# Sample queries and keys projected during the LRU out-projection, out-projection chunks in the order 2, 0, 1, and the first attention head's tiles loaded in the gate path

## Chip, core and metric

One NeuronCore of one Trainium2 chip. The metric is the device time of one execution in microseconds (us), lower is better; for a kernel on one core this is the span of its instructions and about 1.6 us around it.

## What is computed

One inference step of a decoder trunk of four layers, for a prompt of 1024 tokens and for 8 sample sequences of 4 new tokens each (32 rows), all in float32. Layer 0 and 3 are gated convolutions, layer 1 is an RG-LRU, layer 2 is differential attention with a paged cache of 2048 past tokens for each sample sequence. Cut to what matters here:

```python
for i in range(4):
    up = xp * (1 + scale_p) + shift_p        # prompt  (1, 1024, 1024)
    us = xs * (1 + scale_s) + shift_s        # sample  (8, 4, 1024)
    if i == 1:
        op, osm = rglru(up) @ r_w_out, rglru(us) @ r_w_out
    if i == 2:
        q, k, v, z = split(u @ d_w_in)       # 1024 columns each; q and k rotated
        o = softmax(q k_past.T, q k_new.T) @ v    # 8 heads, two score maps each
        o = subln(o) * silu(z) @ d_w_out
    xp = layer_norm(alpha * xp + gate_p * op)
    xs = layer_norm(alpha * xs + gate_s * osm)
```

The sample rows are attended against `cache_k` and `cache_v` (64 MB each is read), the prompt rows against themselves.

## The kernel before

Tokens are columns: 1024 prompt tokens and 32 sample tokens in three chunks of 384, 384 and 288 columns (`CH`); the sample tokens are the last 32 columns of chunk 2. Every large product is made of three float32r products (high x high, high x low, low x high), so a chunk of one output block is 24 matmuls (`gemm_chunk`, L127).

`boundary` closes a layer: `out_proj` multiplies chunk 0, 1, 2 by the eight column blocks of the output weights (eight gemms of 24 matmuls for each chunk), adds the residual that it reads back from DRAM (`xr`, L284), and yields the chunk; `norm` then transposes it, takes the statistics, and `modulate` transposes it back and writes the next layer's input `u` in two parts and, for layer 2, the sample columns once more into `self.us` (L260). The weights (`wo`) are loaded while the first chunk is computed. All weights pass through a ring of two raw buffers of 512 KB (`raw`, tag "raw"): a DMA fills one, ScalarE and VectorE split it into high and low part (L111, L112; L1003, L1004), and only then is the buffer free for the next DMA.

`attn_layer` follows. `qkv` makes six passes of 512 columns (q, q, k, k, v, v); each has eight prompt tiles of 128 tokens, 24 matmuls of 512 columns each (L1060), and loads the next pass's weights meanwhile. In the first pass, after tiles 1 to 4, it also fetches the weights of passes 0 to 3 a second time, raw (`wq_0s` to `wq_3s`, L992, 16 DMAs of 512 KB), multiplies the sample rows with them (`sample_half`, L1012, products in 32-column groups of the array, four instructions for each DMA), sums the four groups with a matmul by `sel` (`sample_rows`, L1036), rotates, and transposes into `qsb` and `ksb`. Beside `qkv`, a second generator `sample_keys` reads the pages of `cache_k` (POOL's queue, 256 DMAs of 256 KB), transposes them on VectorE (`kt`, L1444) and multiplies them with the sample queries (`sps`, L1388) in 16 bursts. `merge` interleaves the two by estimated costs. `zpath` makes the gate (`zz`, 24 chunks), still beside `sample_keys`. Then `heads` does the prompt attention, head by head: it loads keys and queries of a head twice into raw tiles (`tok`, L1150), values `V` (L1157), splits them on ScalarE and POOL (`ks`, `qhl`), and beside it `sample_values` reads `cache_v` (`vp`, 128 DMAs of 512 KB on SP's queue) and multiplies (`sacc`, L1492).

The order on each engine is not the program's. The tile framework takes the instructions with the program's order as priority and lets a simulated timeline choose the next ready one for each engine; it fixes the order before the run, and each engine and each DMA queue then runs it strictly in order. Buffers are handed out in program order within a ring. PSUM banks are handed out by `deal`: three banks P, one Q, three R, one U.

## Time and profile before

| | us |
|---|---|
| time, median of 3 runs | 2441.85 (2439.98 to 2446.5) |
| the profiled execution | 2443.42 |
| its span | 2441.8 |
| PE busy | 2297.3 (94%) |
| VectorE (DVE) busy | 1469.6 (60%) |
| ScalarE (ACT) busy | 910.1 (37%) |
| POOL busy | 341.7 (14%) |

The stretches of the span that this document is about: the LRU's out-projection from 817 to 920, `qkv` from 920 to 1382, `zpath` to 1510, `heads` from 1510 to about 1880, all in us from the span's start. A busy share is read together with the idle time and its releaser: an engine that is idle elsewhere costs nothing, and PE's own idle time does.

### The profile page before, as it was taken

What the parts mean: (1) busy time and instruction counts of PE and PEld (TensorE: products, weight loads), DVE (VectorE), ACT (ScalarE), POOL (GpSimd) and SP (SyncE); (2) the same over time, 40 slices, a digit from 0 to 9 for tenths busy, and PEclk for the clock granted to TensorE, in tenths of its full rate; (3) what the DMA queues carried; (4) which work ended last, traced back from release to release, by engine and by line L of the source; (5) the groups of instructions that cost most, each with busy time, mean ns of one, the idle gap of its engine ahead of it and who ended that gap; (6) DMA issues with size and microseconds to landing.
All of it is one profiled execution on the core that took longest, in us unless ns stands there. A gap on an engine that the chain in (4) does not pass through costs nothing.

```text
span 2441.8 us, 45387 instructions
## 1 busy us (share of the span) xinstructions
PE 2297.3 (94%) x17288; PEld 1952.8 (80%) x17288; DVE 1469.6 (60%) x3047; ACT 910.1 (37%) x1874; POOL 341.7 (14%) x541
## 2 busy tenths in 40 slices
PE   7999999999999998998989997889898999999997
PEld 4989999997888995466656786555566999999997
DVE  5866665467555555555654553676676477666655
ACT  4333333245555233111111111666665254333410
POOL 0200000001010001222223222333321000000000
PEclk9999999999999998999999998999999999999999
DMA  9243335334344425656768765999992321222442
GB/s 327 80 141 105 96 113 164 119 97 124 119 138 130 147 83 185 211 180 211 234 200 271 235 216 170 294 283 293 294 320 87 100 93 53 70 62 71 123 132 75
DMA packets 289392, 393.42 MB, mean 161 GB/s; under 512 B 18749, under 2 KB 197054, under 8 KB 289174
## 3 DMA queue, kind: packets, MB, share of 16 engines
q1 hardware_dynamic: 268694, 323.40, 43.3%
q0 software_dynamic: 20480, 67.13, 8.8%
q8 instruction: 136, 2.23, 0.4%
q14 instruction: 82, 0.67, 0.1%
HBM read 331.14 MB, written 59.31 MB: 160 GB/s over the span
## 4 chain that ended last, share of the span: by engine, by line
PE 67%; issue 13%; DMA 10%; POOLq 4%; DVE 2%; POOL 2%; ACT 1%; SPq 1%; DVEq 0%; ACTq 0%
PE op L127 15%; PE inX L605 12%; PE inZ L605 6%; DMA vp<-cache_v 4%; PE xb L127 4%; PE z L127 4%; PE in L127 3%; POOLq L1347 3%; PE inY L605 3%; PE ada L195 3%; DMA tok<-qd 2%; PE in L726 2%; PE in L641 2%; PE qk L1060 2%; PE zz L127 2%
## 5 line engine op out<-in xcount | busy, mean ns | idle before, releaser
L1060 PE MATMUL qk<-wq,ua 128*128 128x512 f32 x1152 | 289.6, 408 | 2.5 <-DVE wq L1004 2.5
L1060 PEld LDWEIGHTS qk<-wq,ua 128*128 128x128 f32 x1152 | 218.8, 193 | 72.1 <-issue 18.2
L1444 DVE STREAM_TRANSPOSE kt<-kp 128x512 f32<-128x512 f32 x256 | 171.3, 696 | 127.4 <-DMA kp<-cache_k 95.1
L1354 POOL DMA_DIRECT2D kp<-cache_k x256 | 140.4, 548 | 391.8 <-DVE kt L1444 262.5
L1177 PE MATMUL S<-ks,qhl 128*128 128x512 f32 (+2 forms) x384 | 109.9, 396 | 24.5 <-issue 12.3
L1229 ACT ACTIVATE P<-S,rr 128x512 f32<-128x512 f32 (+2 forms) x192 | 110.5, 581 | 49.7 <-DVE rr L1217 26.7
L287 DVE SCALAR_TENSOR_TENSOR r<-op,gate,xr 128x384 f32<-128x384 f32 (+1 forms) x96 | 54.3, 570 | 116.8 <-PE op L127 79.6
L1177 PEld LDWEIGHTS S<-ks,qhl 128*128 128x128 f32 x384 | 61.3, 198 | 60.1 <-ACT P L1229 24.6
L1492 PE MATMUL sacc<-vp,pv 128*16 128x256 f32 x1024 | 81.2, 395 | 24.1 <-DMA vp<-cache_v 23.8
L127 PEld LDWEIGHTS z<-ub,wrz 128*128 128x128 f32 x576 | 92.6, 188 | 11.7 <-issue 10.1
L127 PE MATMUL z<-ub,wrz 128*128 128x384 f32 (+1 forms) x576 | 98.2, 326 | 0.0
L1064 ACT ACTIVATE qkr<-qk 128x512 f32<-128x512 f32 x48 | 28.4, 594 | 186.1 <-PE qk L1060 146.9
L127 PEld LDWEIGHTS zz<-ua,wz 128*128 128x128 f32 x576 | 93.6, 190 | 3.6 <-issue 3.4
L127 PE MATMUL zz<-ua,wz 128*128 128x384 f32 (+1 forms) x576 | 96.1, 326 | 0.0
L1270 PEld LDWEIGHTS pv<-V,wt 128*128 128x128 f32 x576 | 75.8, 198 | 23.0 <-ACT wt L1262 11.6
L127 PEld LDWEIGHTS xb<-ub,wrx 128*128 128x128 f32 x504 | 80.9, 188 | 12.7 <-issue 9.2
L1388 PE MATMUL sps<-kt,qbd 32*32 32x512 f32 x2048 | 86.2, 625 | 4.1 <-DVE kt L1444 2.7
L1270 PE MATMUL pv<-V,wt 128*128 128x128 f32 x576 | 84.5, 289 | 4.3 <-ACT wt L1262 3.6
L324 POOL TENSOR_TENSOR rs<-mv,mhalf 128x1 f32<-128x1 f32 (+1 forms) x36 | 19.2, 540 | 494.5 <-DVE mv L322 489.0
L127 PE MATMUL xb<-ub,wrx 128*128 128x384 f32 (+1 forms) x504 | 87.8, 328 | 0.0
L195 PE MATMUL ada<-wada,ct 128*32 128x512 f32 x384 | 82.5, 616 | 4.3 <-DMA wada<-w_ada 3.1
L127 PE MATMUL op<-ub,ua 128*128 128x384 f32 (+1 forms) x504 | 85.5, 326 | 0.0
(488 smaller groups left out, 5176.0 us busy)
## 6 DMA issues: line engine op xcount, KB each, us to landing
kp<-cache_k POOLq DMA_DIRECT2D x256, 256.0 KB, 3.7
vp<-cache_v SPq DMA_DIRECT2D x128, 512.0 KB, 10.0
wada<-w_ada SPq DMA_DIRECT2D x96, 512.0 KB, 4.2
xa<-xat SPq DMA_DIRECT2D x64, 192.0 KB, 2.2
wra<-a_w_in SPq DMA_DIRECT2D x24, 512.0 KB, 4.1
wrb<-a_w_in SPq DMA_DIRECT2D x24, 512.0 KB, 4.1
xr<-xa SPq DMA_DIRECT2D x64, 192.0 KB, 2.5
tok<-kd SPq DMA_DIRECT2D x32, 256.0 KB, 9.6
```

The source lines that it names most:

```text
L127: nc.tensor.matmul(ps[:, :n], wt[:, wp, k], self.ucols(units[k], up, c), start=i == 0, stop=i == 3 * KB - 1)
L195: nc.tensor.matmul(ps[c : c + 32, :], self.ct[:, k], wts[k // 2][:, k % 2], start=k < 4, stop=k >= 4, tile_position=(0, c),)
L605: nc.tensor.matmul(B[tgt][jj][:, :QH], w[n][:, wp, k], mov[k](jj, up), start=new and m == 0, stop=m == 11, skip_group_check=not new)
L1060: nc.tensor.matmul(ps, u[k][:, c0 : c0 + 128], wq[n, k // 2][:, wp, k % 2], start=i == 0, stop=i == 3 * KB - 1)
L1177: nc.tensor.matmul(st[:, o : o + w], qs[h, g][:, part, s, 128 * qj : 128 * qj + 128], ks[h][:, s, l0 : l0 + w], start=part == 0, stop=part ...
L1229: nc.scalar.activation(p[:, o : o + w], x["S"][s][i][:, :w], AF.Exp, scale=-1.0, bias=rr[:, 6 + s : 7 + s], accum_out=rr[:, c : c + 1])
L1270: nc.tensor.matmul(x["pv"], x["w"][kb // 4][:, j : j + 128], V[h][:, kb], start=kb == 0, stop=kb == qb)
L1347: ld, (r,) = nc.values_load_multi_w_load_instructions(self.ptab[0:1, idx : idx + 1], engines=[et], min_val=0, max_val=159)
L1354: d = eng.dma_start(t, a[src].rearrange(pat)[bass.ds(r, 1), :, cs].rearrange("a p f -> p (a f)"))
L1388: nc.tensor.matmul(ps[b][32 * g : 32 * g + 32, r], qf[rows, f, g, k], kt[rows, g, k], start=f == 0 and k == 0, stop=f == 1 and k == 3, til ...
L1444: nc.vector.transpose(ktv[:, :, j], ring.pop(0).rearrange("p (f t) -> p f t", t=32))
L1492: nc.tensor.matmul(acc[32 * g : 32 * g + 16, :], pt[:k, j, g], vv[:k, :, g], start=j == 0, stop=j == NPG, tile_position=(0, 32 * g))
```

## The change

`sample_qk`, a generator, takes over the sample queries and keys (passes 0 to 3) from `qkv`; the sample values (passes 4 and 5) stay. It is handed to `out_proj` as `hook` and advanced once before each output block of the second and third chunk; each of its 16 steps fetches one raw weight piece of 512 KB and multiplies the one fetched before. The chunk order of this out-projection becomes 2, 0, 1, so that the sample columns are normalised and modulated after the first chunk; the first pass of `qkv` takes its tiles in the order 6, 7, 0 to 5. `rope`, `qsb` and `ksb` move to a pool opened ahead of the out-projection, `sel` to the constants. During the out-projection PSUM is dealt as four banks for transposes, three for gemms and one for the samples, and the ring `xat` shrinks from 6 to 4. In `attn_layer` the keys are interleaved from the second prompt tile instead of the fourth. `heads` yields once after the loads of its first head (`keys(0, 0)`, `queries(0, 0)`, `keys(0, 1)`), and that part is issued after 20 of the 24 chunks of `zpath`, in a pool `ppa` of its own.

```diff
-    def out_proj(self, l, wout, yu, wu):
+    def out_proj(self, l, wout, yu, wu, order, hook):
...
-        for c in range(3):
+        for ci, c in enumerate(order):
...
+                if ci > 0:
+                    next(hook, None)
                 xt = self.sm(f"xr{l}_{c}_{d}", tag="xr")
                 nc.sync.dma_start(xt[:, :n], xa[d][:, c0 : c0 + n])
                 ps = self.gemm_chunk(wts[d], yu, c, f"op{l}_{c}_{d}")
...
+    def sample_qk(self):
...
+        def fetch():
+            if todo:
+                n, j = todo.pop(0)
+                raws.append(self.raw([128, 2, 512], f"wq{n}_{j}s"))
+                nc.sync.dma_start(raws[-1], wv[:, 2 * j : 2 * j + 2, 512 * n : 512 * n + 512])
+
+        def rows(n, pr):
+            kind, m = "qk"[n // 2], n % 2
+            ps = self.bank("acc", f"qss{n}")
+            nc.tensor.matmul(ps, self.sel, pr, start=True, stop=True)
...
+        fetch()
+        done = None
+        for n in range(4):
+            if done:
+                rows(*done)
+            acc = self.bank("acc", f"qs{n}")
+            for j in range(4):
+                fetch()
+                raw = raws.pop(0)
+                for k in (2 * j, 2 * j + 1):
+                    c = 32 * (k % 4)
+                    nc.tensor.matmul(
+                        acc[c : c + 32, :], self.us[:, k], raw[:, k % 2], start=k < 4, stop=k >= 4,
+                        tile_position=(0, c))
+                yield
+            pr = self.tmp.tile([128, 512], F32, tag="spr", bufs=1, name=f"qsp{n}")
+            nc.scalar.copy(pr, acc)
+            done = n, pr
+        rows(*done)
...
-                prompt_tile(n, t)
-                if n == 0 and 1 <= t < 5:
-                    for e in range(2):
-                        fetch(t - 1, 2 * e, "s")
-                        fetch(t - 1, 2 * e + 1, "s")
-                        sample_half(t - 1, e)
-                    sample_rows(t - 1)
-                if n > 3 and t == 0:
+                prompt_tile(n, (6, 7, 0, 1, 2, 3, 4, 5)[i] if n == 0 else i)
+                if n > 3 and i == 0:
...
-        for _ in range(3):
-            next(g)
-        merge(g, 45 * 5120.0, keys, self.shares[0] * KEY_COST)
+        next(g)
+        merge(g, 47 * 5120.0, keys, self.shares[0] * KEY_COST)
...
-        merge(self.zpath(u), 8 * 10.2 * NT, keys, self.shares[1] * KEY_COST)
+        z, ztot = self.zpath(u), 8 * 10.2 * NT
+        merge(itertools.islice(z, 20), ztot, keys, self.shares[1] * KEY_COST)
+
+        cpa, self.ppa = self.pool("ppa", reuse_waits="tile")
+        hs = self.heads(u)
+        next(hs)
+        merge(z, ztot, keys, self.shares[1] * KEY_COST)
...
-            boundary(1, a["r_w_out"][0], A, B)
+            self.bufs = dict(bufs, xat=4)
+            self.deal(tp="PPPU", mm="RRR", acc="Q")
+            boundary(1, a["r_w_out"][0], A, B, (2, 0, 1), self.sample_qk())
```

## Rows read from the trace of the kernel before

**Rows 1.** Busy time by stage: window, length, engines' busy time, PE clock, DMA.

```profile
core 0: us, PE busy (x) PEld busy (x) DVE busy (x) ACT busy (x) POOL busy (x), PEclk, DMA share, GB/s
850.00:889.00 39.00, 39.00 (x243) 38.72 (x242) 18.67 (x39) 12.53 (x22) 1.58 (x3) 1.00 0.25 80
889.00:920.00 31.00, 31.00 (x242) 30.96 (x242) 19.01 (x53) 13.62 (x24) 1.59 (x3) 1.00 0.27 85
920.00:960.00 40.00, 32.38 (x146) 20.55 (x145) 21.60 (x68) 15.81 (x28) 4.88 (x14) 0.90 0.47 143
960.00:1018.00 58.00, 48.45 (x271) 21.15 (x270) 21.46 (x54) 6.84 (x12) 11.51 (x21) 0.86 0.75 241
1510.00:1522.00 12.00, 0.18 (x1) 0.21 (x2) 0.52 (x2) 1.05 (x2) 3.32 (x4) 0.58 1.03 292
1522.00:1840.00 318.00, 279.70 (x2273) 177.61 (x2274) 227.27 (x594) 215.04 (x661) 103.74 (x72) 0.95 1.02 295
```

**Rows 2.** Stage table of L1012 (sample products of passes 0 to 3) alone.

```profile
920.00:1018.00 98.00, 20.24 (x64) 2.42 (x64) 0.88 0.63 201
```

**Rows 3.** Stage table of L1036 (sum of the four groups) alone.

```profile
920.00:1018.00 98.00, 5.48 (x8) 1.61 (x8) 0.88 0.63 201
```

**Rows 4.** PE's waits in 920 to 1018: total, times, longest.

```profile
PE qs L1012 <- DMA wq_3s<-d_w_in: 9.6, 3, 3.9
PE qs L1012 <- DMA wq_0s<-d_w_in: 3.8, 1, 3.8
```

**Rows 5.** Stage tables of L1060 (prompt tiles) alone, two stretches.

```profile
920.00:1018.00 98.00, 40.99 (x145) 28.39 (x146) 0.88 0.63 201
...
1018.00:1382.00 364.00, 248.15 (x1007) 190.36 (x1008) 0.97 0.68 218
```

**Rows 6.** Timeline of PE at full clock: start, length, instruction, count.

```profile
1201.07 1.05 PE L1012 MATMUL qs<-wq_1r,us 128*32 128x512 f32 x4
1202.05 5.13 PE L1060 MATMUL qk<-wq,ua 128*128 128x512 f32 x21
...
1230.90 0.62 PE L1012 MATMUL qs<-wq_2r,us 128*32 128x512 f32 x2
...
1231.89 5.61 PE L1060 MATMUL qk<-wq,ua 128*128 128x512 f32 x23
```

**Rows 7.** SP's queue: its waits over the whole span.

```profile
SPq L992 <- PE qs L1012: 31.8, 12, 6.4
```

**Rows 8.** DMA issues in 920 to 1018: count, KB each, us to landing.

```profile
wq_0s<-d_w_in SPq DMA_DIRECT2D x4, 512.0 KB, 4.8
```

**Rows 9.** Timeline at the out-projection's start and in its third chunk.

```profile
823.00 0.45 DVE L97 TENSOR_TENSOR ua<-rsz,ua 128x288 fp32r<-128x288 f32 x1
...
836.03 1.23 DVE L112 TENSOR_TENSOR ub<-wo_7r,ub 128x1024 fp32r<-128x1024 f32 x1 [2.86 <-ACT ub L111]
...
900.87 6.08 PE L127 MATMUL op<-ua,ub 128*128 128x288 f32 x44
```

**Rows 10.** Query of the tile `us`: when its eight copies ran.

```profile
L260 POOL COPY us<-u x8: 209/209/210, 937.0 to 947.9; 128x32 f32<-128x32 f32 x8
```

**Rows 11.** Timeline after the out-projection: last weight split, first `cache_k` page.

```profile
928.27 1.23 DVE L1004 TENSOR_TENSOR wq<-wq_3r,wq 128x1024 fp32r<-128x1024 f32 x1 [1.10 <-ACT wq L1003]
...
958.88 0.75 POOL L1354 DMA_DIRECT2D kp<-cache_k  x1 [9.06 <-PE qs L1012]
```

**Rows 12.** The page's costliest groups: transposes of the `cache_k` pages.

```profile
L1444 DVE STREAM_TRANSPOSE kt<-kp 128x512 f32<-128x512 f32 x256 | 171.3, 696 | 127.4 <-DMA kp<-cache_k 95.1
```

**Rows 13.** Timeline where `zpath` ends and `heads` begins.

```profile
1511.93 1.72 SPq L1150 DMA_DIRECT2D tok<-qd  x2
...
1516.00 0.37 SPq L1157 DMA_DIRECT2D V<-vd  x1
...
1520.67 1.04 ACT L1170 CAST qhl<-tok 128x1024 fp32r<-128x1024 f32 x1 [10.67 <-DMA tok<-qd]
...
1521.82 0.98 PE L1177 MATMUL S<-ks,qhl 128*128 128x256 f32 x3 [12.26 <-issue]
```

More of the change, by code (lines that the diff above doesn't have):

```diff
@@ L158, in setup @@
         self.us = cp.tile([128, KB, S], F32, name="us")
+        self.sel = cp.tile([128, 128], F32, name="sel")
+        for g in range(4):
+            nc.vector.tensor_reduce(
+                self.sel[:, 32 * g : 32 * g + 32], self.ident.rearrange("p (g j) -> p j g", g=4), axis=AX.X, op=ALU.add)
         self.gate = [cp.tile([128, KB, NV], F32, name=f"gate{i}") for i in range(3)]
@@ L297, in out_proj @@
                 rt.append(r)
-                if c == 2 and d == 7:
+                if ci == 2 and d == 7:
                     yield c, rt, False
@@ L318, in norm @@
             ps = [first[i] if first else self.half(l, c, i, rt, 0, self.tp)]
-            ps.append(self.half(l, c, i, rt, 1, self.mm if c == 2 and i >= 1 else self.tp))
+            ps.append(self.half(l, c, i, rt, 1, self.mm if first and i >= 1 else self.tp))
             mv = self.stp.tile([128, 4], F32, tag="mv", bufs=2, name=f"mv{l}_{c}_{i}")
@@ L974, in attn_consts @@
         )
-        self.sel = cp.tile([128, 128], F32, name="sel")
-        for g in range(4):
-            nc.vector.tensor_reduce(
-                self.sel[:, 32 * g : 32 * g + 32], self.ident.rearrange("p (g j) -> p j g", g=4), axis=AX.X, op=ALU.add)
         self.coef = cp.tile([128, NB], F32, name="coef")
@@ L982, in attn_consts, with rotate @@
         self.ots = cp.tile([128, KB, S], F32, name="ots")
+    def rotate(self, rt, w, t, pool, bufs):
+        nc = self.nc
+        rv = rt[:w].rearrange("p (s f) -> p s f", f=64)
+        x = rv[:, :, 0:16]
+        tt = []
+        for q in range(2):
+            r = pool.tile([128, 8, 16], F32, tag="rp", bufs=bufs, name=f"rp{rt.name}_{q}")
+            nc.vector.tensor_tensor(
+                r[:w], x, self.rope[:w, q, t : t + 1, :].to_broadcast([w, 8, 16]), ALU.mult
+            )
+            tt.append(r)
+        nc.vector.tensor_tensor(rv[:, :, 0:8], tt[0][:w, :, 0:8], tt[1][:w, :, 8:16], ALU.add)
+        nc.vector.tensor_tensor(rv[:, :, 8:16], tt[0][:w, :, 8:16], tt[1][:w, :, 0:8], ALU.add)
@@ new lines, in sample_qk @@
+    def sample_qk(self):
+        nc, a = self.nc, self.a
+        wv = a["d_w_in"][0].rearrange("(k p) f -> p k f", p=128)
+        todo = [(n, j) for n in range(4) for j in range(4)]
+        raws = []
+        def fetch():
[7 more added lines that the diff above has]
+            nc.tensor.matmul(ps, self.sel, pr, start=True, stop=True)
+            rt = self.tmp.tile([128, 512], F32, tag="sr", bufs=1, name=f"qsr{n}")
+            nc.scalar.mul(rt, ps, -0.125 if kind == "q" else 1.0)
+            self.rotate(rt, 128, 8, self.tmp, 2)
+            if kind == "k":
+                nc.sync.dma_start(
+                    a["k_sample"][0, :, :, 8 * m : 8 * m + 8, :].rearrange("b t s f -> (b t) (s f)"), rt[:S]
+                )
+            dst = self.qsb if kind == "q" else self.ksb
+            nc.vector.transpose(dst[:, 16 * m : 16 * m + 16].rearrange("p f t -> p (f t)"), rt)
+        fetch()
[17 more added lines that the diff above has]
+        rows(*done)
@@ L1285, in begin @@
                 [128, 20], F32, tag="rr", bufs=6, name=f"rr{h}_{qb}"))
+        keys(0, 0)
+        queries(0, 0)
+        keys(0, 1)
+        yield 0
         self.cmask = self.pp.tile([128, 512], F32, name="cmask")
@@ L1568, in main @@
         def main():
-            hs = self.heads(u)
             while True:
@@ L1616, in filler_for, with boundary @@
             return filler
-        def boundary(l, wout, y, u):
+        def boundary(l, wout, y, u, order=(0, 1, 2), hook=iter(())):
             first = None
-            for c, rt, full in self.out_proj(l, wout, y, u):
+            for c, rt, full in self.out_proj(l, wout, y, u, order, hook):
                 if not full:
+                    for _ in hook:
+                        pass
+                    self.deal(tp="PPPQ", mm="RRRU")
                     first = [self.half(l, c, i, rt, 0, self.tp) for i in range(3)]
@@ L1678, in run @@
             self.bufs = bufs
+            cs, sp = self.pool("smq", side="right")
+            self.rope = sp.tile([128, 2, 9, 16], F32, name="rope")
+            nc.sync.dma_start(self.rope, a["rope"])
+            self.qsb = sp.tile([128, 32, S], F32, name="qsb")
+            self.ksb = sp.tile([128, 32, S], F32, name="ksb")
             ct, self.tmp = self.pool("tmpm", reuse_waits="tile", side="right")
-            boundary(1, a["r_w_out"][0], A, B)
-        cms = [ct, cb]
+            self.bufs = dict(bufs, xat=4)
+            self.deal(tp="PPPU", mm="RRR", acc="Q")
+            boundary(1, a["r_w_out"][0], A, B, (2, 0, 1), self.sample_qk())
         if self.layers > 2:
-            for cm in cms:
+            for cm in (ct, cb):
                 cm.__exit__(None, None, None)
@@ L1692, in run @@
             self.attn_layer(2, A)
-            for cm in (cr, cc):
+            for cm in (cr, cc, cs):
                 cm.__exit__(None, None, None)
```

53 lines of the change are left out of this document (13 added, 40 removed).

## Prediction, made before the changed kernel ran

> **What bounds the kernel now.** I read the table of busy time by stage first. In the second and third chunk of the LRU's out-projection PE is busy all the time at the full clock, while the DMA engines work at about a quarter [rows 1]: this stretch is bound by PE, and whatever PE is given there lengthens it, but a DMA there is nearly free. Right behind it, from 920 to 1018, PE is busy for 32.4 of 40 and 48.5 of 58 us: 17.2 us are idle, and the granted clock falls to 0.90 and 0.86, that is, part of the work runs at 1.2 instead of 2.4 GHz [rows 1]. The list of PE's waits names the reason for most of it: 13.4 us in four waits of the sample products for raw weight pieces [rows 4], while the DMA share has risen to 0.75 [rows 1]. From 1510 to 1522 PE does nothing but 0.18 us of work, and the heads behind it run with saturated DMA engines, 295 GB/s at a share of 1.02 [rows 1]. So the change touches a PE-bound stretch, a stretch where PE waits for DMAs and the clock suffers, and one where DMA is the limit.
>
> The sum is made against the profiled execution, 2443.42 us (span 2441.8); the median of the runs shown is 1.57 us lower, and I take the differences over to it.
>
> **What goes away behind the out-projection.** The sample products cost 20.2 us of PE there [rows 2], the eight instructions of the group sums 5.5 us [rows 3], the waits 13.4 us [rows 4]: 39.1 us together. Two things more hang on it. The prompt tiles in that stretch take 40.99/145 = 0.283 us a matmul, later 248.15/1007 = 0.246 [rows 5]: 145 x 0.037 = 5.4 us lost to gaps and to the low clock. Without the waits the clock should stay up; I take 4 us of the 5.4 (bounds 0 and 5.4).
>
> **What the out-projection gets.** Sixteen steps of four instructions. At full clock such a step lasts from 1201.07 to the next instruction at 1202.05, 0.98 us; eight of these instructions, when two steps fall together, last from 1230.90 to 1231.89, 0.99 us [rows 6]. A step thus has a price that does not depend on its size: twice the work in the same time. The change advances one step before each output block, with a gemm between, so I take the single price, 16 x 0.98 = 15.7 us; if the planner pairs them all it is 7.9 us. The group sums are 5.5/8 = 0.69 us each [rows 3], at low clock in part; I take 4 us for eight. Added: 20 us (bounds 10 and the 25.7 of the old place). All of it is on the path, since PE has no idle time there.
>
> The Trainium skill, TensorEngine Tiling, section "Tiling Modes" (Key Properties), says that a change of the tiling mode, as against another tile in the same mode, drains TensorE. The pair of rows above agrees, as far as it goes. By that rule alone, without the rows, one would set each of the 16 steps at its full price and count on no pairing, which is the value that I take.
>
> **The waits of the new place.** A step multiplies what was fetched one step earlier, and there are two raw buffers. A piece lands 4.8 us after its issue in the busy stretch [rows 8], and DMA is quieter in the new place; an output block of 24 matmuls lies between two steps, at 6.08/44 = 0.138 us for 288 columns already 3.3 us [rows 9], more for 384. A fetch has two such blocks of time, over 6.6 us, against 4.8. So few waits: I take 4 us in all (0 to 13.4, the old place's).
>
> The sample columns must be there first. Now `us` is written between 937.0 and 947.9 [rows 10], 17 to 28 us after the last gemm at 920. In the new order the same chain starts after the first chunk, 8 x 3.3 = 27 us after 817, so `us` comes at about 861 to 872, in the second half of the next chunk; the first four steps gather there, the others follow one for each block. The fetches wait for it in their buffers, but the residual loads `xr` stand behind the next fetch in SP's queue; that is the first rival below.
>
> **The chunk order.** The gated product's last 288 columns are split only at 823.45 [rows 9], and these columns are now wanted first. The first seven inputs of the first gemm need 21 x 0.138 = 2.9 us from 817, so PE lacks work from 820 to 823 unless the planner starts another block: I take 2 us (0 to 4). The weights keep up: the last one is split at 837.3, and with 3.3 us for a block the eighth begins at 817 + 7 x 3.3 = 840 [rows 9]. The transposes of the last chunk are 384 instead of 288 columns wide, but the sum over the chunks stays, and the five tiles 6, 7, 0, 1, 2 (24 x 0.246 = 5.9 us each) cover the end of the chain, 28 us, with 30 us.
>
> **The weights of the first pass.** Three of the four pieces are loaded ahead now; the last is split at 929.5, 9 us after the last gemm [rows 11]. With the change both raw buffers hold sample pieces until the last step, one block before the end. From then on four pieces go through two buffers, each with a landing of 4.8 us [rows 8] and a split of 2.3 us (ScalarE 1.04 for a cast of that size [rows 13], then VectorE 1.23 [rows 11]): two rounds, 14 us, of which 4 to 9 us lie beside the last gemms. The last piece is split 5 to 10 us after the last gemm, about as now, but the second and third come later too. I take 4 us (0 to 12).
>
> **The keys.** Pages start at 958.88, 39 us after the last gemm [rows 11]; with no sample DMAs ahead of the page table in SP's queue and with an earlier place in the interleaving this gap should shrink to some 30 us. That covers the later end of the out-projection in part; the pages are no bound later (256 transposes of 0.7 us, 171.3 us of VectorE over 550 us [rows 12]). Taken at nothing; the cover is that PE has the prompt tiles to do meanwhile. If it is gone, the third rival's price holds.
>
> **The heads.** The query load goes out at 1511.93 and lands for the split at 1520.67, PE starts at 1521.82 after 12.3 us of idling [rows 13]. The loads move into the gate path, which has PE-bound time left. But the heads are bound by DMA: what leaves their stretch for certain is the query tile and `V` of the first head, 0.5 MB each, 1.05 MB / 295 GB/s = 3.6 us [rows 1, 13]. Between that and the 12.3 us I take 6 (0 to 12.3). `sel` in the constants, the smaller ring `xat` and three gemm banks instead of four I take at nothing: PE has its gemms queued around them.
>
> **Sum.** -39.1 - 4 + 20 + 4 + 2 + 4 - 6 = -19.1 us: 2424.3 for the profiled execution, 2422.7 against the median. I say 2422. All bounds to the good side: -39.1 - 5.4 + 10 - 12.3 = -47, 2395; all to the bad: -39.1 + 25.7 + 13.4 + 4 + 12 = +16, 2458.
>
> **Rivals.** First, slower: SP's queue. The fetch of a step waits for the buffer that PE frees one step before, and it stands ahead of the residual load of the block that PE does next. SP has waited for PE's sample products twelve times, 31.8 us in total, 2.65 us each [rows 7]. If such a wait holds up the residual load in each of the sixteen steps, PSUM does not come free and PE stands still: 16 x 2.65 = 42 us instead of 4, 2422 + 38 = 2460. It decides from (19 + 4) / 16 = 1.4 us a step on. Against it: two buffers, and blocks of over 3.3 us between. The Trainium skill, DMA: Bandwidth & Descriptors, section "Anatomy of one DMA", says that a DMA engine never waits on a semaphore and that the issuing sequencer does. That speaks for this rival, and by it the blocked fetch holds all that is behind it; SP's row shows such waits. Chance 0.12.
>
> Second, the first pass's weights come late: 12 us instead of 4, 2422 + 8 = 2430. For it: the ring is taken to the end. Against: the planner sees it and has the transposes to fill in. Chance 0.14.
>
> Third, the keys set the end of `qkv` and `zpath`: VectorE waits 95.1 us for pages [rows 12]. Then the 43 us that go away are given back as waits for pages; what counts is the pages' start, 26 us later with the out-projection's end and 9 us earlier by the shorter gap, less 6 us in the heads: 2442 + 26 - 9 - 6 = 2453. Against it: PE, not VectorE, is busy nearly all of that stage. Chance 0.08.
>
> Fourth, the change doesn't do what it says: the planner, which takes whatever is ready in its simulated time, moves the sample steps behind the last gemm again, and only the heads gain: 2442 - 4 = 2438. Chance 0.06.
>
> Chance of the forecast: 0.60, with its own range 2402 to 2440.
>
> **How the numbers follow.** About 0.3%, 7 us, is what a measurement of this kernel can tell from no change: faster is below 2434.5, slower above 2449.2. Faster: 0.55 of the 0.60, 0.11 of the second rival, 0.02 of the fourth: 0.68. Slower: the first rival, 0.05 of the third: 0.17. Within: 0.15. The range 2400 to 2450 leaves out the first rival and half of the third, and a little at the good end.
>
> **What would show it.** Right: no waits for `wq_*s` of more than some 4 us in all in the out-projection; its end at 940 to 946 instead of 920; by the time that six prompt tiles and one burst are done, about 20 us ahead of 1018; clock above 0.95 right behind the out-projection; the first matmul of the heads within 4 us after `zpath`. Wrong: PE idle before `op` in chunks 0 and 1 with SP waiting for the sample products (first rival); PE waiting for `wq_2r` and `wq_3r` (second); `sps` waiting for `kt` or `kp` (third); sample products after the last `op` (fourth).

## Result and profile after

| | before | after |
|---|---|---|
| time, median | 2443.71 us (2439.98 to 2446.5, 4 runs) | 2418.24 us (2412.42 to 2423.53, 4 runs) |
| ratio | 1 | 0.9896, 95% interval 0.9869 to 0.9924 |
| profiled execution | 2443.42 us | 2418.05 us |
| mean granted clock | 0.975 | 0.985 |

The changed kernel is 25 us faster, where 19 to 20 were predicted. Six points that both kernels pass, read from the traces (start of the last or first matmul of the group), show where the gain arises and where part of it goes:

| | before | after | gained since the start |
|---|---|---|---|
| last gemm of the out-projection | 920.0 | 942.5 | -22.5 |
| 212 to 215 matmuls of prompt tiles and the first burst of the keys done | 1035.0 | 1012.4 | 22.6 |
| last prompt tile of `qkv` | 1382.0 | 1362.5 | 19.5 |
| last gemm of `zpath` | 1509.3 | 1497.4 | 11.9 |
| last `sacc` of the heads | 1841.9 | 1825.0 | 16.9 |
| first gemm of layer 2's out-projection with `ub1a` | 1882.1 | 1857.7 | 24.4 |

So the sample move wins 45.1 us behind the out-projection for 22.5 in it; `zpath` then gives back 7.6, and the heads win 12.5. Of the 3.1 us lost in the rest of `qkv`, some 2 are no loss: by 1035.0 the kernel before had done three prompt matmuls (0.27 us each) and ten transposes `qkf` (26 in 3.81 us against 16 in 2.40) more than the changed one by 1012.4; the rest I have not traced. The heads' 12.5 us fall into 5.0 up to the last `sacc` and 7.5 behind it, where 12 instead of 22 instructions of the scores (`S`) are left. Other runs split the same sum in other ways, so only the sum is read below.

The stretch behind the out-projection in a table of busy time by stage of the changed kernel (window, length, PE, PEld, DVE, ACT and POOL busy with their instructions, granted clock, DMA share, GB/s), to be held against the two stretches from 920 to 1018 in [rows 1]:

```profile
942.80:1012.40 69.60, 66.04 (x415) 48.43 (x413) 43.80 (x99) 26.81 (x40) 14.68 (x27) 1.00 0.61 188
```

PE is idle for 3.6 us instead of 17, and its clock is 1.00 instead of 0.90 and 0.86: all of this work now runs at 2.4 GHz. PE's waits from 817 to 1013 in the changed kernel, against [rows 4]:

```profile
PE rt L315 <- DVE r L294: 2.5, 1, 2.5
PE qk L1099 <- ACT wq L1066: 2.2, 4, 0.9
PE qk L1099 <- DVE wq L1067: 1.3, 3, 0.5
```

No sample product waits for a raw piece any more. SP does: its queue's waits in the same stretch have the line that answers to [rows 7].

```profile
SPq L1011 <- PE qs L1038: 15.0, 8, 3.4
```

15 us of blocked fetches, and none of it reaches PE in the out-projection: its one wait, the 2.5 us for `r`, ends at 829.49, ahead of the first sample step at 873.82.

What `zpath` gives back stands in PE's waits from 1380 to 1530 of the changed kernel, in the first of these two lines; the second belongs to the heads' start, where before there was the one wait of 12.3 us [rows 13]:

```profile
PE zz L127 <- DVE zt L1165: 8.3, 2, 6.2
PE S L1210 <- DVE zt L1165: 5.9, 1, 5.9
```

A gemm of the gate waits for a gate tile `zt` on VectorE. The longest of these waits, 6.2 us, followed back through the timelines (start, length, instruction, in brackets the idle time before it and its releaser; lines of POOL, ACT, DVE and PE, in this order):

```profile
1436.57 0.54 POOL L1388 DMA_DIRECT2D kp<-cache_k  x1 [1.52 <-DVE zt L1165]
1452.28 2.65 POOL L1198 TENSOR_TENSOR ks<-tok,ks 64x512 fp32r<-64x512 f32 x2 [15.17 <-ACT ks L1195]
1454.87 1.64 POOL L1388 DMA_DIRECT2D kp<-cache_k  x3
...
1451.09 1.05 ACT L1195 CAST ks<-tok 128x1024 fp32r<-128x1024 f32 x1 [6.37 <-DMA tok<-kd]
...
1447.21 3.68 DVE L1476 STREAM_TRANSPOSE kt<-kp 128x512 f32<-128x512 f32 x6 [1.23 <-PE sps L1420]
1458.84 0.71 DVE L1476 STREAM_TRANSPOSE kt<-kp 128x512 f32<-128x512 f32 x1 [7.95 <-DMA kp<-cache_k]
...
1464.56 0.52 DVE L1165 SCALAR_TENSOR_TENSOR zt<-zt,zz 128x384 f32<-128x384 f32 x1
...
1465.13 7.11 PE L127 MATMUL zz<-ua,wz 128*128 128x384 f32 x30 [6.17 <-DVE zt L1165]
```

At 1447.2 VectorE takes the six pages that have landed, which frees their buffers; POOL could issue the next pages at once. But the first head's key subtraction, which the change has moved here, stands ahead of them in POOL's queue and waits for ScalarE's cast, which waits for the load of the keys. The pages go out only at 1454.87, VectorE waits 7.95 us for the first of them, the gate's `zt` stands behind the transposes of three pages on VectorE, and PE waits 6.17 us for `zt`. Four engines, one late load.

The 5.9 us at the heads' start have another late load behind them, that of the causal mask `cmask`, which leaves SP's queue at 1498.76 (two lines of DVE, one of PE):

```profile
1502.75 0.30 DVE L1250 CUSTOM_DVE_ANT_0 S<-S,cmask 128x128 f32<-128x128 f32 x1 [7.26 <-DMA cmask<-cmask]
...
1503.32 0.41 DVE L1165 SCALAR_TENSOR_TENSOR zt<-zt,zz 128x256 f32<-128x256 f32 x1
...
1503.88 1.83 PE L1210 MATMUL S<-ks,qhl 128*128 128x256 f32 x6 [5.91 <-DVE zt L1165]
```

VectorE's first masking of scores waits 7.26 us for it, and the last `zt` stands behind that. POOL has no part in this one.

### The profile page after: what moved, and what is told of

It is laid out like the page before. It is cut to its first block, busy times and chain, and to the rows that moved or that the text cites. A ratio compares the mean times of both kernels' runs of the same rounds, so it can differ in the third digit from the quotient of the medians.

```text
span 2416.3 us, 45377 instructions
## 1 busy us (share of the span) xinstructions
PE 2279.6 (94%) x17288; PEld 1948.7 (81%) x17288; DVE 1470.0 (61%) x3047; ACT 911.0 (38%) x1874; POOL 338.3 (14%) x541
## 5 line engine op out<-in xcount | busy, mean ns | idle before, releaser
L127 PEld LDWEIGHTS zz<-ua,wz 128*128 128x128 f32 x576 | 95.9, 193 | 12.5 <-DVE zt L1165 9.0
L127 PE MATMUL op<-ua,ub 128*128 128x384 f32 (+1 forms) x504 | 89.7, 333 | 0.0
L127 PEld LDWEIGHTS op<-ua,ub 128*128 128x128 f32 x504 | 81.9, 192 | 9.1 <-issue 9.0
```

Source lines behind the costliest of these rows:

```text
L127: nc.tensor.matmul(ps[:, :n], wt[:, wp, k], self.ucols(units[k], up, c), start=i == 0, stop=i == 3 * KB - 1)
```

## Experiments

A ratio is taken to runs of the kernel before on the same chip. Single runs of one kernel spread by 10 to 20 us and more, so the traces' milestones are read beside the medians.

**The two halves apart.** The sample move alone, with the heads' loads where they were:

```diff
-        keys(0, 0)
-        queries(0, 0)
-        keys(0, 1)
-        yield 0
...
+        keys(0, 0)
+        keys(0, 1)
+        queries(0, 0)
         blocks = [(h, qb) for h in range(8) for qb in range(8)]
```

> The changed kernel with the loads of the first attention head put back behind the gate path; only the sample queries and keys are moved, in the chunk order 2, 0, 1. Theory (POOL's queue): the sample move alone is worth what the milestones of the first burst of the keys show, about 22 us, and nothing of it is lost in the gate path, because the wait of 6 to 8 us of the gate's gemms for the gate's tiles comes from the subtraction of the first head on POOL, which is gone here: 2421 to 2424 us, ratio about 0.991, end of the gate path about 20 us earlier than before, and the heads' first matmul again 12 us behind it. Rival (the keys are short of time whatever POOL does, since they start later against TensorE): the waits in the gate path stay, the end of the gate path is only 12 us earlier, and the time is about 2432 us, ratio 0.995.

Measured: 2426.12 us, ratio 0.993 (0.9907 to 0.9953), some 17 to 18 us gained: a time between the theory's 2421 to 2424 and the rival's 2432. The trace decides. The last gemm of `zpath` starts at 1488.9, 20.4 earlier than before, and of PE's waits for a gate tile there is one of 1.0 us left:

```profile
PE S L1210 <- issue: 12.1, 1, 12.1
...
PE zz L127 <- DVE zt L1165: 1.0, 1, 1.0
```

The wait at the heads' start is back, those for `zt` are all but gone: the loss in `zpath` belongs to the heads' loads. And the other half, the loads in the gate path of the kernel before:

```diff
-        merge(self.zpath(u), 8 * 10.2 * NT, keys, self.shares[1] * KEY_COST)
+        z, ztot = self.zpath(u), 8 * 10.2 * NT
+        merge(itertools.islice(z, 20), ztot, keys, self.shares[1] * KEY_COST)
+        cpa, self.ppa = self.pool("ppa", reuse_waits="tile")
+        hs = self.heads(u)
+        next(hs)
+        merge(z, ztot, keys, self.shares[1] * KEY_COST)
```

> The kernel before with only the loads of the first attention head moved into the gate path. Theory (POOL's queue): the heads gain about 12.7 us, and the gate path gives back about 8 of it, because the subtraction on POOL stands ahead of the pages of the key cache there too: 2438 to 2440 us, ratio 0.998, with a wait of the gate's gemms of 6 us or more. Rival (the loss belongs to the later keys of the sample move): no such wait, 2431 us, ratio 0.995. The prediction's term for this part was -6 us.

Measured: 2437.32 us, ratio 0.9976 (0.9959 to 0.9994), 6 to 7 us gained. Its profiled execution, 2444.55 us, is one of its longest, so only the pattern is read from the trace. It is the same, in a kernel whose keys are hardly later than before (first `sps` at 991.5 against 989.4; waits of PE, then POOL's timeline):

```profile
PE S L1177 <- DVE zt L1132: 6.7, 1, 6.7
...
PE zz L127 <- DVE zt L1132: 5.2, 1, 5.2
```

```profile
1453.22 0.54 POOL L1356 DMA_DIRECT2D kp<-cache_k  x1 [0.82 <-issue]
1475.16 2.64 POOL L1165 TENSOR_TENSOR ks<-tok,ks 64x512 fp32r<-64x512 f32 x2 [21.40 <-ACT ks L1162]
1477.75 1.64 POOL L1356 DMA_DIRECT2D kp<-cache_k  x3
```

The 5.2 us end the chain over POOL and the pages (VectorE waits 8.03 us for one), the 6.7 us that over the mask (VectorE waits 8.09 us for `cmask`). Both runs put the loss on the heads' loads and speak against the rival that the keys are late because of the sample move. The halves add up: 17 to 18 and 6 to 7, against 25.

**Where in the queues the loss sits.** Four attempts to take the stop away. First, the loads later:

```diff
-        merge(itertools.islice(z, 20), ztot, keys, self.shares[1] * KEY_COST)
+        merge(itertools.islice(z, 23), ztot, keys, self.shares[1] * KEY_COST)
```

> The changed kernel with the first head's loads issued after 23 of the 24 chunks of the gate path instead of 20. Theory (POOL's queue): the subtraction on POOL then stands behind more of the pages, the wait in the gate path falls to 3 us or less, but the loads come up to 3 chunks (about 12 us) later and the heads start some 5 us later after the gate path: 2412 to 2418 us. Rival (keys short of time in any case): the wait in the gate path stays, the heads start later too, 2420 to 2425 us.

Measured: 2422.06 us, ratio 0.9906 (0.988 to 0.9933), no difference from the changed kernel; the time lies in the rival's range, and the waits stay (8.1 and 4.3 us). But the subtraction starts at 1454.23 instead of 1452.28 and has the same neighbours in POOL's queue: the place in the program didn't move it, presumably because the planner puts an instruction where its data are ready in the simulated time. The edit did not do what both theories had expected of it, so it says little on either. Second, the subtraction on VectorE:

```diff
-                nc.gpsimd.tensor_tensor(lo, t[oth, s], lo.bitcast(F32), ALU.subtract)
+                eng = nc.vector if h == 0 else nc.gpsimd
+                eng.tensor_tensor(lo, t[oth, s], lo.bitcast(F32), ALU.subtract)
```

(and likewise for the first queries.)

> The changed kernel, but the subtractions that make the low parts of the first head's first keys and queries run on VectorE instead of POOL, so that nothing stands ahead of the pages of the key cache in POOL's queue. Theory (POOL's queue): the waits of the gate's gemms for the gate's tiles (16.5 us in all, 8.3 for the zt tile in two) shrink to under 2 us, and the time is 2410 to 2413 us against 2418 of the changed kernel. Rival (the keys are short of time in any case): the waits stay, 2418 us. Third possibility: VectorE's own queue now waits for the same loads, the gate's tiles stand behind that, and the loss only changes its place: 2418 to 2424 us.

Measured: 2430.29 us, ratio 0.9935 (0.9909 to 0.9962): the third possibility, and worse than its 2418 to 2424. VectorE's own waits have a new line, and POOL's page now waits for VectorE:

```profile
DVE ks L1199 <- ACT ks L1195: 12.9, 2, 6.7
```

```profile
1454.45 0.55 POOL L1390 DMA_DIRECT2D kp<-cache_k  x1 [17.84 <-DVE kt L1478]
```

The stop has only changed its engine. The time, though, is not lost there: from the last prompt tile to the last gemm, `zpath` takes 130.9 us against 134.9 in the changed kernel, and the heads take 375.0 from there to layer 2's out-projection against 360.3. Why the heads are longer I have not traced. Third and fourth, raw buffers for the first head's loads apart from those of the gate's weights, issued after 20 and after 8 chunks:

```diff
-            t = self.raw([128, 2, 512], f"tok{q}{h}_{g}")
+            if h == 0 and (q == 1 or g == 0):
+                t = self.ppa.tile([128, 2, 512], F32, tag="tok", bufs=2, name=f"tok{q}{h}_{g}")
+            else:
+                t = self.raw([128, 2, 512], f"tok{q}{h}_{g}")
```

and in the fourth also

```diff
-        merge(itertools.islice(z, 20), ztot, keys, self.shares[1] * KEY_COST)
+        merge(itertools.islice(z, 8), ztot, keys, self.shares[1] * KEY_COST)
```

> The changed kernel with two raw buffers of their own for the first head's keys and first queries, so that these loads no longer wait behind the gate's weights for the shared raw buffers. Theory (an in-order queue is stopped by an instruction whose data come late, because the load waits for a raw buffer that the gate's weights hold): the stop of 15 us in POOL's queue ahead of the subtraction shrinks to under 5, the pages of the key cache keep coming, the gate's gemms wait under 3 us for the zt tile instead of 8.3 + 5.9, and the time is 2408 to 2413 us. Rival (the pages or VectorE are the limit at the end of the gate path in any case): the waits stay or move to another tile, 2416 to 2424 us.

> The changed kernel with the first head's keys and first queries in two raw buffers of their own and their loads issued after 8 of the 24 chunks of the gate path instead of 20. Theory (a load that comes late stops ScalarE, and the gate's tiles stand behind its cast; it comes late because at the end of the gate path SP's queue holds the gate's stores, which wait for those very tiles): this early in the gate path the loads land before their casts' turn, the gate's gemms wait under 4 us for the zt tile instead of 8.3 + 5.9, the heads follow the gate path without a gap, and the time is 2408 to 2413 us. Rival (VectorE and the pages of the key cache limit the gate path, and what the heads' loads take from it is given back wherever they stand): the waits of the gate's gemms stay at 8 us or more, 2416 to 2424 us.

Measured: 2429.34 us, ratio 0.9932 (0.9907 to 0.9957), and 2434.69 us, ratio 0.9966 (0.9946 to 0.9987). Both are worse than the changed kernel and above the rivals' 2416 to 2424. In both the chain of the changed kernel returns at an earlier place. In the first the planner now lets the loads go out from 1373.34 on; that of the second keys follows at 1387.77, right behind the subtraction that frees the first keys' buffer, and the next subtraction stands ahead of the pages (POOL, DVE, PE):

```profile
1394.06 2.59 POOL L1201 TENSOR_TENSOR ks<-tok,ks 64x512 fp32r<-64x512 f32 x2 [6.32 <-ACT ks L1198]
1396.60 1.62 POOL L1391 DMA_DIRECT2D kp<-cache_k  x3
...
1399.60 0.71 DVE L1479 STREAM_TRANSPOSE kt<-kp 128x512 f32<-128x512 f32 x1 [10.83 <-DMA kp<-cache_k]
...
1403.92 11.32 PE L127 MATMUL zz<-ua,wz 128*128 128x384 f32 x48 [12.55 <-DVE zt L1165]
```

At the end of its gate path the pages keep coming, but ScalarE's casts wait 7.84 and 7.08 us for loads that stand behind the gate's stores in SP's queue, the gate's own tanh stands behind the casts on ScalarE, VectorE waits for the tanh, and at the end of that chain PE waits 7.83 us for ScalarE's `sc`. In the second run it is the same chain as above; the load of the second keys goes out at 1393.49, again right behind the subtraction that frees the first keys' buffer:

```profile
1399.70 2.59 POOL L1201 TENSOR_TENSOR ks<-tok,ks 64x512 fp32r<-64x512 f32 x2 [6.24 <-ACT ks L1198]
1402.24 1.62 POOL L1391 DMA_DIRECT2D kp<-cache_k  x3
...
1405.98 2.01 DVE L1479 STREAM_TRANSPOSE kt<-kp 128x512 f32<-128x512 f32 x3 [11.43 <-DMA kp<-cache_k]
...
1409.76 10.65 PE L127 MATMUL zz<-ua,wz 128*128 128x384 f32 x48 [12.08 <-DVE zt L1165]
```

So it is not enough to take the buffers from the gate's weights: with two buffers for three loads, the second keys wait for the first keys' buffer, and my theory was too narrow there. What all of them share is a compute instruction that depends on a fresh load, in an engine's queue ahead of the stream of pages or gate tiles. The last run takes that away: only the loads are issued in the gate path, and the casts and subtractions come behind the last page in POOL's queue, because their target `ks` is now taken from the pool that is opened behind the keys. It changes more than that: the two loads have two raw buffers of their own, they are issued after 18 chunks instead of 20, and the load of the second keys stays behind the gate path.

```diff
-                ks[h] = self.ppa.tile([128, 2, T], F32R, tag="ks", bufs=self.n_ks, name=f"ks{h}")
+                ks[h] = self.pp.tile([128, 2, T], F32R, tag="ks", bufs=self.n_ks, name=f"ks{h}")
...
-        keys(0, 0)
-        queries(0, 0)
-        keys(0, 1)
+        pre[1, 0, 0] = twice(1, 0, 0)
+        pre[0, 0, 0] = twice(0, 0, 0)
+        values(0)
         yield 0
+        keys(0, 0)
+        queries(0, 0)
+        keys(0, 1)
```

(`keys` and `queries` take these tiles from `pre`; `values` is the load of `V`.)

> The changed kernel, but only the loads of the first head's first keys, first queries and values are issued in the gate path (after 18 of its 24 chunks, into two raw buffers of their own); the high parts and the subtractions on POOL come behind the last page of the key cache in POOL's queue. Theory (POOL's queue: the subtraction stands ahead of pages, waits for a late load, and pages, kt, zt and TensorE wait behind it): no gemm of the gate path waits for a zt tile over 2 us, the gate path is as long as in the run with the sample move alone, 123 us instead of 135, the heads' first matmul follows within 5 us, and the time is 2408 to 2414 us. Rival (the loads themselves, their place in SP's queue and the shared DMA engines cost the gate path what the heads gain): waits of 8 us or more for zt, kt or the gate's weights stay, 2416 to 2424 us.

Measured: 2411.91 us, ratio 0.9856 (0.9827 to 0.9886), in the theory's range and the fastest of all kernels here, though its interval overlaps that of the changed kernel. Its waits of PE from 1362 to 1500, and PE's timeline where the changed kernel waits 6.17 us and where `zpath` ends:

```profile
PE spt L1463 <- ACT sc L1451: 3.6, 2, 2.2
PE zz L127 <- DVE zt L1165: 3.0, 2, 2.8
...
PE S L1219 <- POOL ks L1207: 0.8, 1, 0.8
```

```profile
1450.92 20.30 PE L127 MATMUL zz<-ua,wz 128*128 128x384 f32 x120
...
1487.78 5.53 PE L127 MATMUL zz<-ua,wz 128*128 128x384 f32 x36
1493.14 0.48 PE L1219 MATMUL S<-ks,qhl 128*128 128x256 f32 x2
1494.46 1.38 PE L1219 MATMUL S<-ks,qhl 128*128 128x256 f32 x6 [0.84 <-POOL ks L1207]
```

Where the changed kernel did 72 gate matmuls and then waited, this one does 120 without a stop. The first keys' load goes out at 1449.27, later than the changed kernel's 1446.01, so it is not an earlier load that helps, but that nothing in POOL's queue waits for it ahead of the pages; the next page goes out at 1452.14, 1.1 us after VectorE has begun on the six that have landed. The heads begin in the gate path's last gemm and go on after a gap of 0.84 us. The 5.9 us of the mask are gone too, since `cmask` leaves SP's queue at 1491.69 (VectorE waits 2.7 us for it, PE not at all).

The forecast did not come out whole: a wait of 2.8 us for `zt` is left where under 2 was expected, and `zpath` lasts from 1363.9 to 1493.0, 129 us where 123 was expected and 135 it was. A gain of 6 us in `zpath` alone could come from the planner's order (see the chunk order below), so the case rests on the rows and not on the time: with the dependent instructions behind the pages this stop is gone, ahead of them it is there in five kernels (the changed one, the heads alone, the later loads, own buffers and the early loads).

**What a sample step costs.** Steps in pairs:

```diff
                         tile_position=(0, c))
-                yield
+                if j % 2:
+                    yield
```

> The changed kernel with the sample steps taken in pairs: eight visits of eight instructions instead of sixteen of four. Theory (a visit has a price of about 1 us whatever its size): some 12 visits lie in the out-projection of the changed kernel, eight would cost 4 us less, so its last gemm ends at about 939 instead of 942.7 us and the time falls to about 2414 us. Rival (the pieces come too late for pairs: a visit now needs both raw buffers, and the next two pieces can only be fetched behind it, 4.8 us against a block of about 4 us): TensorE or SP waits 1 to 2 us for each visit, the last gemm ends at 942 to 950 us, and the time is 2418 to 2426 us.

Measured: 2421.34 us, ratio 0.9898 (0.9872 to 0.9924); the out-projection's last gemm at 941.9. The time lies in the rival's range, but neither mechanism came. No sample product waits, and the planner puts the same visits into the out-projection as for the changed kernel, four single steps, a pair, two single ones, a pair, and so on, as the pieces arrive; the program's pairing isn't what makes a pair. How a single step, a pair and a step that was cut in two look, in PE's timeline of the changed kernel:

```profile
885.84 1.05 PE L1038 MATMUL qs<-wq_3s,us 128*32 128x512 f32 x4
886.83 4.29 PE L127 MATMUL op<-ua,ub 128*128 128x384 f32 x23
...
895.01 0.62 PE L1038 MATMUL qs<-wq_0s,us 128*32 128x512 f32 x2
895.02 0.62 PE L1038 MATMUL qs<-wq_1s,us 128*32 128x512 f32 x2
...
921.80 1.04 PE L1038 MATMUL qs<-wq_2s,us 128*32 128x512 f32 x2
922.78 0.55 PE L241 MATMUL xt<-ident,xn 128*128 128x128 f32 x3
```

A single step uses two of the array's four column groups (`c` is 0 and 32 or 64 and 96); in a pair the products of two pieces start 0.01 us apart, on different groups, and half a step, on one group alone, takes the 0.98 us of a whole one (921.80 to 922.78). So the time goes with the columns that one group gets, and not with the number of groups. That suggested another cut of the pieces:

```diff
-                nc.sync.dma_start(raws[-1], wv[:, 2 * j : 2 * j + 2, 512 * n : 512 * n + 512])
+                f, k0 = 512 * n + 256 * (j // 2), 4 * (j % 2)
+                nc.sync.dma_start(raws[-1], wv[:, k0 : k0 + 4, f : f + 256])
...
-                for k in (2 * j, 2 * j + 1):
-                    c = 32 * (k % 4)
...
+                f, e = 256 * (j // 2), j % 2
+                for k in range(4):
+                    nc.tensor.matmul(
+                        acc[32 * k : 32 * k + 32, f : f + 256], self.us[:, 4 * e + k], raw[:, k], start=e == 0,
+                        stop=e == 1, tile_position=(0, 32 * k))
```

> The changed kernel with another cut of the raw sample pieces: a piece of 512 KB holds four row blocks by 256 columns instead of two by 512, so that each sample step uses all four 32-column groups of the array at once instead of two. First theory (the price of 0.98 us of a step is that half of the array's column groups lie idle; products on different groups run side by side, as the starts 895.01 and 895.02 of two pieces in one visit of the changed kernel show): a step falls to about 0.55 us, the sample products of the out-projection from 14.0 to about 8 us, its last gemm ends at about 937 instead of 942.7 us, and the time is 2411 to 2414 us. Second theory (the prediction's reading: a step has a fixed price, whatever its size, for going over to the 32-column tiles and back): a step stays at 0.9 to 1.0 us, the last gemm ends at 942 to 943, and the time is 2416 to 2422 us.

Measured: a step lasts 892.57 - 892.00 = 0.57 us, where the changed kernel's takes 0.98, and two steps in one visit 903.67 - 902.67 = 1.00:

```profile
892.00 0.64 PE L1039 MATMUL qs<-wq_3s,us 128*32 128x256 f32 x8
892.57 0.66 PE L315 MATMUL rt<-ident,r 128*128 128x128 f32 x4
...
902.67 0.64 PE L1039 MATMUL qs<-wq_0s,us 128*32 128x256 f32 x8
903.13 0.61 PE L1039 MATMUL qs<-wq_1s,us 128*32 128x256 f32 x8
903.67 0.44 PE L241 MATMUL xt<-ident,xn 128*128 128x128 f32 x2
```

The first theory holds for the step: 0.41 of the 0.98 us were idle column groups. Of a fixed price for a visit the rows leave 0.57 - (1.00 - 0.57) = 0.14 us. The Trainium skill, TensorEngine Tiling (Array Packing), section "Tiling Modes" (Key Properties), says that different tiles can work in parallel, beside the rule on the drain that the prediction cited. The two starts 0.01 us apart agree with the first; what a drain costs here no run shows by itself, but it would have to fit into the 0.14 us. The out-projection's last gemm falls to 939.1 (937 was expected), but the time does not: 2421.98 us, ratio 0.9927 (0.9905 to 0.9949). The last steps run ahead of their pieces (PE waits 1.0 and 0.8 us for the last two), and the first pass's weights are no earlier: from the last gemm to the end of the first burst it takes 72.6 us instead of 69.6, at a clock of 0.95 instead of 1.00, with 5.0 us of idling instead of 3.6, and the burst ends at 1011.9 instead of 1012.4. At layer 2's out-projection the two traces are level, 1857.2 and 1857.7.

**SP's queue.** The fetch ahead taken out:

```diff
-        fetch()
         done = None
         for n in range(4):
```

> The changed kernel without the fetch ahead: each sample step fetches the piece that it multiplies itself. Theory (the planned order issues a fetch as soon as a raw buffer is free, wherever it stands in the program, so that SP's waits lie beside the gemms): the last gemm still ends within 3 us of 942.7, 2416 to 2422 us. Rival (the prediction's first, SP's queue): the step waits for its own piece, about 4.8 us less what the block hides, and the residual loads stand behind the fetches: 16 x 2.65 = 42 us more in the out-projection, about 2460 us; half of that if every other step is hidden.

Measured: 2419.12 us, ratio 0.9892 (0.9861 to 0.9922). The gemms of the out-projection reach from 825.8 to 946.7, 120.9 us, against 122.4 in the changed kernel; no wait for a piece. The first rival's 42 us are nowhere.

**The chunk order alone**, in the kernel before:

```diff
-            boundary(1, a["r_w_out"][0], A, B)
+            boundary(1, a["r_w_out"][0], A, B, (2, 0, 1))
```

> The kernel before with only the chunk order 2, 0, 1 in the out-projection and the tile order 6, 7, 0 to 5 in the first pass; the sample queries and keys stay behind the out-projection. Theory (the prediction's): the order costs 2 us (0 to 4) at the start of the out-projection, because the gated product's last 288 columns come late, and nothing else changes: its last gemm ends at 921 to 924 instead of 920.3 us, 2444 to 2448 us. Rival (the earlier sample columns also take away waits behind the out-projection): the waits of the sample products for raw pieces fall by half, 2436 to 2440 us.

Measured: 2437.26 us, ratio 0.9962 (0.9944 to 0.998), 8 us faster; slower by 2 was expected. The last gemm of the out-projection starts 3.3 us later (923.3). The term had 2, but for another reason: PE has no wait at 820 to 823, since the planner did start another block; 0.5 us are there when the first gemm starts (817.5 instead of 817.0), and 1.0 is a wait for `r` at 847. The time lies in the rival's range, but the sample products wait 12.0 us for pieces instead of 13.4, where it had them fall by half, so the rival is not it. By the last prompt tile both kernels are level (1382.1 and 1382.0). The gain arises later, in stretches that the edit doesn't touch: 3.2 us in `zpath` (last gemm 1506.1 instead of 1509.3), 2.9 more up to layer 2's out-projection (1876.0 instead of 1882.1). The planner has put the rest of the program in another order. Why that order is better I have not traced; it says that differences of some 6 us in `zpath` and the heads can come from the planner's order alone, and I claim none smaller in these stretches.

**Both ideas together**, the pieces of four row blocks and the early loads in buffers of their own:

> Both of the last two: the pieces of four row blocks, and the first head's loads early with raw buffers of their own. First theories of both: 6 us less in the out-projection and 5 to 10 us less at the gate path, 2402 to 2408 us. If both rivals hold: 2416 to 2424 us. If one of them holds: 2408 to 2414 us.

Measured: 2435.86 us, ratio 0.9975 (0.996 to 0.999), above all three forecasts. The out-projection's last gemm is at 938.2, and `zpath` lasts from 1361.0 to 1510.3, as long as with the early loads alone: the loss in the gate path came along, and the gain in the out-projection did not show in the time.

## Why the prediction was right, step by step

The time came out 4 us below the forecast of 2422, by a sum of which several terms were off and made up for each other: the clock, the first pass's weights, the out-projection and the heads came out 3.5 to 6.5 us better each, some 19 together, and the steps left behind and `zpath` some 11 worse. That the total is so near is in part luck.

- **Sample work and waits behind the out-projection, -39.1.** Right in kind. The waits for pieces are gone. Of the products 2.10 us and of the sums 1.02 us stay behind the last gemm, since the planner leaves the last two steps there (942.91 and 944.70), the fourth rival's sign for two of sixteen: 3.1 us that the sum had not allowed for.
- **Clock and gaps, -4 (0 to 5.4).** Mis-sized, and its bound was no bound: it counted the prompt tiles alone. They fell from 57.80/215 = 0.269 to 53.36/212 = 0.252 us a matmul, 3.6 us; but the first burst of the keys had lost time as well. It has 128 instructions in both kernels and took 9.37 us before and 4.36 after (tables by stage of the burst alone, and a piece of it in PE's timeline; before, then after):

```profile
920.30:1035.00 114.70, 9.37 (x128) 1.67 (x128) 0.00 (x0) 0.00 (x0) 0.90 0.63 198
...
1001.10 1.98 PE L1388 MATMUL sps<-kt,qbd 32*32 32x512 f32 x24
```

```profile
942.80:1012.40 69.60, 4.36 (x128) 2.10 (x128) 0.00 (x0) 0.00 (x0) 1.00 0.61 188
...
1008.04 4.46 PE L1420 MATMUL sps<-kt,qbd 32*32 32x512 f32 x128
```

  Before, the burst was cut into six pieces by sample products and prompt matmuls, and from 990 to 1010 the granted clock was 0.82 and 0.83; after, it runs in one piece at 1.00. That is 5.0 us more: 8.6 in all instead of 4. How much of the 5.0 is the clock and how much the cutting, no run separates.
- **Weights of the first pass, +4.** They cost 2.2 + 1.3 = 3.5 us of waits. But they took the place of 3.6 us of other waits in that stretch of the kernel before (2.8 for `qkr`, 0.8 for `u`), which the sum had not counted as removed. Net idle time fell by 17.2 - 3.6 = 13.6 us, where the sum had 13.4 - 4 = 9.4. The second rival does not hold.
- **Sixteen steps and the sums in the out-projection, +20.** Measured 12.65 us for fourteen of the sixteen steps and 3.06 us for six of the eight sum instructions, 15.7. The price of 0.98 for a single step was right as a number; three pairs came, which I had set at none. The reading that it is a price whatever the size was wrong: it goes with the columns that a group gets, 0.98 to 0.99 us for 512 on one, two or four groups and 0.57 for 256 on four, of which 0.14 may be fixed.
- **Waits in the new place, +4 (0 to 13.4).** None for pieces: the lower end. The run without the fetch ahead shows that even that reserve wasn't needed.
- **Chunk order, +2; `sel`, `xat` and three gemm banks, nothing.** The order alone measures 3.3, though not by the wait that the term had. In the changed kernel PE waits another 2.5 us for `r` in the first chunk, which the run of the order alone, with its four gemm banks, doesn't have there. VectorE's `r` waits for the residual load `xr` in both runs; in the changed one that load goes out at 824.85 instead of 824.24, behind the load of `rope`, and `r` starts at 828.95 instead of 828.36. Behind PE's wait the granted clock of 817 to 850 is 0.95, and 24 matmuls take 4.95 us where the next 24 take 3.43. That the missing fourth bank is the reason is argued from this alone; it wasn't tried by itself, and 0.6 us of the wait may be the load of `rope`. Together with the order some 7 us (22.5 - 15.7) against 2, and with the two items above the out-projection comes to +22.5 against the 26 of the sum.
- **The keys, at nothing.** Here a step failed. I had looked for the pages' start, which was harmless, and not at what the heads' part issues on POOL: the rows of the gate path show that the moved subtraction stops the pages, and 7.6 us of the gain are gone by the end of `zpath`. The prediction had costed the moved loads by their transfer, not by the instructions that come with them and the queues these join.
- **The heads, -6 (-3.6 to -12.3).** Right as a net sum and wrong in its parts. The half alone gives 6 us; but the gross gain is the upper end, 12.5, and the rest is paid back in `zpath`. Up to the last `sacc` the heads won 5.0, near the 3.6 that the DMAs gave for certain; the 7.5 behind it, from scores done earlier, the step had not thought of. With only the loads moved, `zpath` gives back 2.0 instead of 7.6 and the heads win 10.6, and the ratio is 0.9856 against 0.9896, with intervals that overlap.
- **What would show it.** The out-projection's end at 942.9 lay in 940 to 946, the clock right behind at 1.00, no waits for pieces, the first burst 22.6 us earlier instead of some 20. The heads' first two matmuls even begin in the last gemm of `zpath`, but PE then waits 5.9 us, for a gate tile behind the mask.

## What to carry to other kernels

When work is moved, list for each instruction that comes with a load the engine whose queue it joins, and ask what stands behind it there: an in-order queue passes a late load on from POOL to the pages, to VectorE and to TensorE. Move the loads, and leave the instructions that depend on them behind the stream that must not stop. Small loads count too: here a mask cost 5.9 us. And a stall that lowers the clock is to be priced on all the work behind it, not on one kind.

## What the runs showed of the hardware

Products on different 32-column groups of the array run side by side, with starts 0.01 us apart; at 512 columns a group, one, two and four groups take 0.98, 0.98 and 0.99 us of PE, and the same 512 KB of weights take 0.98 us on two groups and 0.57 on four. After a wait of PE of 2.5 us the granted clock of the stretch from 817 to 850 was 0.95 in the changed kernel; after one of 2.4 us in the run without the fetch ahead, and after one of 2.6 us in the run of both ideas, it was 1.00. A short wait may cost the clock or not.
